# Gate columns in one stationary tile, gates of new tokens from a diagonal, decay rows of three heads by transfers

## The chip, the cores and the metric

One core of a Trainium2 chip runs the whole program. The engines are TensorE (PE, matmuls), VectorE (DVE), ScalarE (ACT) and GpSimd (POOL); SyncE (SP) issues most DMA transfers. The metric is the device time of one execution in microseconds; lower is better. Three runs of the kernel before took 1218.15, 1218.84 and 1219.11 us.

## The reference

One layer of a decoder trunk on 512 prompt tokens and 8 new tokens of other sequences: a SwiGLU feed-forward (FFN), a token mixer, a second FFN, each with norms around it. The mixer has two branches of four heads each, retention and gated DeltaNet. What the change touches is the gates of the DeltaNet branch (8 columns of `w_in`, 4 for `ga`, 4 for `gb`) and the decays made from them:

```python
proj = (h @ w_in).astype(f32)
rq, rk, rv, rg, conv_in, gz, ga, gb, gate_r, gate_g = jnp.split(proj, idx, axis=-1)
beta = jax.nn.sigmoid(gb)
g_gdn = -jnp.exp(gdn_a_log.astype(f32)) * jax.nn.softplus(ga + gdn_dt_bias.astype(f32))
...
G = jnp.cumsum(gc, axis=-1)          # within a chunk
dm = decay_masks(G)                  # exp(G_i - G_j) below the diagonal
a_mat = jnp.eye(c, dtype=jnp.float32) + jnp.where(strict, bc[..., :, None] * dm * kk, 0.0)
u_v = lax.linalg.triangular_solve(a_mat, bc[..., None] * vc, ...)
qk = jnp.einsum('nbhid,nbhjd->nbhij', qc, kc) * dm
```

Inputs and outputs are fp32, and everything is computed in fp32 or in two-part splits of it.

## The kernel before

Features lie on the partitions, the 520 tokens on the free axis in two halves of 260 columns. A weight is loaded as `raw`, and split into a high part `whi` (a ScalarE cast, L350) and a rest `wlo` (a VectorE subtraction, L351); the activations `xhl` are split in the same way. A product takes three passes for each tile of 128 features, L408 to L410: high by high, high by rest, rest by high. A pass is one matmul of a 128x128 stationary tile with 260 columns. The feed-forwards save multiplications by seven-product schemes (`sv`, `dn`), which the change leaves alone.

The mixer (L1023) projects in the order of `proj_order`: first GAB, a block of 128 columns of which 8 are the gates and 120 are zeros, then the columns CK, CQ, CV of the four DeltaNet heads, the retention's RQ, RK, RV, and the gating columns. `first_units` (L701) does GAB and head 0's CK together, first half, then second half, while the sums of the norm are still being made: `ss` (L471) adds the squares over the partitions, `rb` (L477) spreads the factor of the norm over the partitions again. The raw result of GAB is scaled by `rb` into `rows` (L1167). `gates` (L1170) transposes `rows`, makes `g` (here `gg`) and `beta` for each token on VectorE and ScalarE, and then one group of matmuls into the bank `gc`: the running sums `G` of the chunks, by the triangle `triu` (L1215), and for the eight new tokens each gate of each head spread over all partitions, by eight matmuls of 8 columns, four for `g` and four for `beta` (L1218).

`gdn_head` (L1368) is a generator, one for each head. `decays` (L1235) spreads head h's `G` over the partitions: four fp32 matmuls, one for a chunk, into the bank `gbc` (L1240). From it ScalarE makes `eg` (L1244), VectorE `DT` (L1247) and `ekd`. Later the head works through its chunks: `ks` (L1447) multiplies the state S, `pS` (L1457) gives its update, which VectorE adds to S (L1459).

The order of the work is written by hand. Projections run as passes, and every 6 passes are a tick (`tick`, L223), some 0.72 us. Generators such as `gdn_head` are spawned beside them, and each `yield n` lets n ticks pass before the generator's next instructions are issued. `LATER`, a table at the head of the file, moves single steps: its entry `("gdn_head", 1): {51: 1, 52: -3}` makes the 51st wait of head 1 a tick longer and the 52nd three shorter, so the entries count the yields of a generator. TURN (48 ticks) keeps the heads apart. Each engine then works its own list strictly in that order.

## Time and profile before

| | |
|---|---|
| time, median of 3 runs | 1218.84 us |
| lowest and highest | 1218.15 and 1219.11 us |
| profiled execution | span 1218.5 us; no time of its own beside the span |
| PE busy | 1189.1 us (98%) |
| DVE busy | 899.6 us (74%) |
| ACT busy | 573.7 us (47%) |
| POOL busy | 277.1 us (23%) |
| matmuls on PE | 9937 |
| granted TensorE clock, mean | 0.990 |

The span goes from the first to the last instruction of the profiled execution. A busy TensorE isn't one at its peak: matmuls overlap, and their ends are modelled, so a matmul is read by the distance from its start to the next one's start. A fp32 matmul appears as two records. The mixer's part that the change touches lies between about 366 and 650 us.

### The profile page before, as it was taken

The numbers are of one execution on the slowest core, as the hardware profiler recorded it, in microseconds if no ns is written. First come the engines' busy times: TensorE is split into PE (matmuls) and PEld (weight loads), VectorE is DVE, ScalarE is ACT, GpSimd is POOL, SyncE is SP. The second block draws the span as 40 slices with busy tenths as digits, with TensorE's granted clock in tenths as the row PEclk, the third lists the DMA queues.
The fourth block names the chain that finished last, engine by engine and source line by source line (L and its number), as shares of the span: only waits on it lengthen the run. The fifth ranks groups of instructions, "written<-read, shape, count | busy, mean of one in ns | idle before, by whom it ended". The sixth has DMA issues, their size and how long they took to land.

```text
span 1218.5 us, 25498 instructions
## 1 busy us (share of the span) xinstructions
PE 1189.1 (98%) x9937; PEld 1176.9 (97%) x9937; DVE 899.6 (74%) x1933; ACT 573.7 (47%) x1195; POOL 277.1 (23%) x502
## 2 busy tenths in 40 slices
PE   8999999999999999999999999999999999999995
PEld 7999999999999999999999999998999999999994
DVE  8988888776548787877666667546888888867554
...
DMA packets 79689, 170.87 MB, mean 140 GB/s; under 512 B 17104, under 2 KB 20016, under 8 KB 79568
## 3 DMA queue, kind: packets, MB, share of 16 engines
...
## 4 chain that ended last, share of the span: by engine, by line
PE 88%; DVE 6%; ACT 2%; issue 1%; DMA 1%; POOL 1%; SPq 0%; DVEq 0%; ACTq 0%; POOLq 0%
PE sv L408 10%; PE sv L409 10%; PE sv L410 10%; PE p L408 7%; PE p L410 7%; PE p L409 7%; PE dn L408 7%; PE dn L409 7%; PE dn L410 7%; DVE wlo L351 2%; PE br L408 1%; PE br L409 1%; PE br L410 1%; PE g L409 1%; PE g L410 1%
## 5 line engine op out<-in xcount | busy, mean ns | idle before, releaser
L408 PE MATMUL p<-xhl,whi 128*128 128x260 f32 x784 | 231.0, 295 | 0.0
L409 PE MATMUL p<-xhl,whi 128*128 128x260 f32 x784 | 222.0, 283 | 1.4 <-DVE xhl L506 1.4
L410 PE MATMUL p<-xhl,wlo 128*128 128x260 f32 x784 | 221.3, 282 | 1.7 <-DVE wlo L351 1.7
L351 DVE TENSOR_TENSOR wlo<-raw,whi 128x1024 fp32r<-128x1024 f32 (+2 forms) x121 | 142.3, 1182 | 37.7 <-ACT whi L350 35.9
L408 PE MATMUL sv<-th,w 128*128 128x260 f32 x592 | 167.2, 282 | 0.5 <-ACT q L833 0.5
L409 PE MATMUL sv<-tl,w 128*128 128x260 f32 x592 | 167.1, 282 | 0.0
L410 PE MATMUL sv<-th,w 128*128 128x260 f32 x592 | 167.0, 282 | 0.0
L409 PEld LDWEIGHTS p<-xhl,whi 128*128 128x128 f32 x784 | 148.4, 189 | 2.0 <-DVE xhl L506 1.8
L410 PEld LDWEIGHTS p<-xhl,wlo 128*128 128x128 f32 x784 | 147.9, 189 | 2.1 <-DVE wlo L351 2.1
L408 PEld LDWEIGHTS p<-xhl,whi 128*128 128x128 f32 x784 | 148.1, 189 | 0.7
L350 ACT CAST whi<-raw 128x1024 fp32r<-128x1024 f32 (+2 forms) x121 | 116.4, 971 | 31.3 <-DMA raw<-dn_in 16.9
L369 DVE TENSOR_TENSOR w<-s,w 128x512 fp32r<-128x512 f32 x148 | 101.5, 688 | 37.9 <-ACT w L368 36.5
L307 POOL DMA_DIRECT2D s<-gu_in x74 | 65.1, 973 | 282.4 <-DMA s<-gu_in 143.8
L410 PE MATMUL dn<-hh,wlo 128*128 128x260 f32 x448 | 126.6, 283 | 1.2 <-DVE wlo L351 1.2
L408 PE MATMUL dn<-hh,whi 128*128 128x260 f32 x448 | 127.0, 283 | 0.0
L409 PE MATMUL dn<-hl,whi 128*128 128x260 f32 x448 | 126.7, 283 | 0.0
L409 PE MATMUL sv<-xhl,w 128*128 128x260 f32 x444 | 125.5, 283 | 0.0
L408 PE MATMUL sv<-xhl,w 128*128 128x260 f32 x444 | 125.4, 282 | 0.0
L410 PE MATMUL sv<-xhl,w 128*128 128x260 f32 x444 | 125.0, 281 | 0.0
L408 PEld LDWEIGHTS sv<-th,w 128*128 128x128 f32 x592 | 111.4, 188 | 0.9 <-ACT q L833 0.7
L410 PEld LDWEIGHTS sv<-th,w 128*128 128x128 f32 x592 | 111.6, 188 | 0.0
L409 PEld LDWEIGHTS sv<-tl,w 128*128 128x128 f32 x592 | 111.2, 188 | 0.0
(408 smaller groups left out, 3230.4 us busy)
## 6 DMA issues: line engine op xcount, KB each, us to landing
...
s<-gu_in SPq DMA_DIRECT2D x74, 256.0 KB, 5.7
s<-gu_in POOLq DMA_DIRECT2D x74, 256.0 KB, 5.4
...
a<-gu_in SPq DMA_DIRECT2D x37, 256.0 KB, 5.9
...
```

The source lines that it names most:

```text
L307: self.nc.gpsimd.dma_start(out=out, in_=term, accum_op=ALU.add)
L350: self.nc.scalar.copy(hi[:, ks], t[:, ks])
L351: self.nc.vector.tensor_tensor(lo[:, ks], t[:, ks], hi[:, ks].bitcast(F32), ALU.subtract)
L369: nc.vector.tensor_tensor(w[:, 1], t[i], w[:, 0].bitcast(F32), ALU.subtract)
L408: mm(ps, hi[:, k, :], xh, start=first, stop=False, skip_group_check=more)
L409: mm(ps, hi[:, k, :], xl, start=False, stop=False, skip_group_check=more)
L410: mm(ps, lo[:, k, :], xh, start=False, stop=last, skip_group_check=more)
```

## The change

GAB is loaded as its 8 columns alone (`gab`, 32 KB and not 512 KB). A stationary tile `both` is filled with zeros by ScalarE, the high parts of the 8 columns go into its columns 0 to 7, and VectorE's rests into 8 to 15. It then takes two passes, by the high and by the low part of the activations, and the result has 16 rows, which are added in pairs in `gates` after the transposes.

For the new tokens `g` and `beta` are multiplied with an identity into a diagonal `dg`, and one matmul with a stationary tile of ones spreads all 64 numbers.

One further matmul gives `G` in rows (16 rows of 128, a row for each chunk and head). They are copied to SBUF and written to DRAM (`gscr`). Heads 1 to 3 have their rows spread by a transfer that SP issues ROWS_EARLY = 12 ticks before the decays; `eg` and `DT` then read SBUF. Head 0 keeps its four matmuls, which now stand in `gdn_head`. The transfer adds a yield to heads 1 to 3, so that the entries of `LATER` meet the yield before the one that they met so far.

```diff
@@ units: the order of the loads
-            out += [("win", i, 0, 8) for i in range(n)]
+            out += [("gab", 0, 0, 8)] + [("win", i, 0, 8) for i in range(n - 1)]
...
@@ load_to
+            elif u[0] == "gab":
+                t = self.slot("gabw", (P, KD, 8))
+                nc.sync.dma_start(out=t, in_=a["gab"])
...
@@ split
+        if self.unit_list[j][0] == "gab":
+            self.load_to(j)
+            t = self.loaded[self.group[j]]
+            both = self.whl.tile([P, KD, P], F32R, tag="w", name=self.name("both"))
+            self.started(j)
+            self.split_done[j] = (both, None)
+            self.nc.scalar.activation(both, self.ones.unsqueeze(1).to_broadcast([P, KD, P]), AF.Copy, scale=0.0)
+            self.nc.scalar.copy(both[:, :, 0:8], t)
+            self.nc.vector.tensor_tensor(both[:, :, 8:16], t, both[:, :, 0:8].bitcast(F32), ALU.subtract)
+            return
...
@@ passes
         mm(ps, hi[:, k, :], xh, start=first, stop=False, skip_group_check=more)
+        if lo is None:
+            mm(ps, hi[:, k, :], xl, start=False, stop=last, skip_group_check=more)
+            return
...
@@ gates
+        sb = c.tile([P, 5, 16], F32, name="gsb")
+        nc.gpsimd.memset(sb, 0.0)
...
-        nc.vector.tensor_tensor(ga[:, 0:4, :], ptv[:, 0:4, 0:4], dt.unsqueeze(1).to_broadcast([P, 4, H]), ALU.add)
-        nc.vector.tensor_tensor(ga[0:DEC, 4, :], ptv[0:DEC, 4, 0:4], dt[0:DEC], ALU.add)
-        nc.vector.tensor_copy(gb[:, 0:4, :], ptv[:, 0:4, 4:8])
-        nc.vector.tensor_copy(gb[0:DEC, 4, :], ptv[0:DEC, 4, 4:8])
+        nc.vector.tensor_copy(sb[:, 0:4, :], ptv[:, 0:4, :])
+        nc.vector.tensor_copy(sb[0:DEC, 4, :], ptv[0:DEC, 4, :])
+        nc.vector.tensor_tensor(ga, sb[:, :, 0:4], sb[:, :, 8:12], ALU.add)
+        nc.vector.tensor_tensor(gb, sb[:, :, 4:8], sb[:, :, 12:16], ALU.add)
+        nc.vector.tensor_tensor(ga, ga, dt.unsqueeze(1).to_broadcast([P, 5, H]), ALU.add)
...
+        diag = self.small("dg", [P, 2, H, DEC])
+        eye = self.ident[0:DEC, 0:DEC].unsqueeze(1).to_broadcast([DEC, H, DEC])
+        for i, src in enumerate((g, beta)):
+            nc.vector.tensor_tensor(diag[0:DEC, i], src[0:DEC, 4, :].unsqueeze(2).to_broadcast([DEC, H, DEC]), eye, ALU.mult)
         yield 13
 
         pc = self.bank("gc")
         nc.tensor.matmul(pc[:, 0:16], self.triu, g[:, 0:4, :], start=True, stop=True)
-        for i, src in enumerate((g, beta)):
-            for h in range(H):
-                nc.tensor.matmul(
-                    pc[:, 16 + (i * H + h) * DEC : 16 + (i * H + h + 1) * DEC],
-                    src[0:DEC, 4, h : h + 1].to_broadcast([DEC, P]),
-                    self.ident[0:DEC, 0:DEC],
...
+        nc.tensor.matmul(pc[0:16, P : 2 * P], g[:, 0:4, :], self.triu, start=True, stop=True)
+        nc.tensor.matmul(pc[:, 16:80], self.ones[0:DEC, :], diag[0:DEC], start=True, stop=True)
+        grow = self.slot("growc", (16, P))
+        nc.vector.tensor_copy(grow, pc[0:16, P : 2 * P])
+        self.gscr = self.dram.tile([NCH, H, P], F32, name="gscr")
+        nc.sync.dma_start(out=self.gscr.rearrange("c h i -> (c h) i"), in_=grow)
...
+    def decay_rows(self, h):
+
+        t = self.slot("gbc", (P, NCH, P))
+        self.nc.sync.dma_start(out=t, in_=self.gscr[:, h, :].unsqueeze(0).to_broadcast([P, NCH, P]))
+        return t
...
@@ gdn_head
-        if turn > self.now:
-            yield turn - self.now
-        eg, DT = self.decays(h)
+        if h:
+            if turn - ROWS_EARLY > self.now:
+                yield turn - ROWS_EARLY - self.now
+            rows = self.decay_rows(h)
+            yield max(turn, self.now + ROWS_EARLY) - self.now
+        else:
+            if turn > self.now:
+                yield turn - self.now
+            rows = self.bank("gbc").rearrange("p (c i) -> p c i", i=P)
+            for i in range(NCH):
+                nc.tensor.matmul(rows[:, i, :], self.g[:, i, h : h + 1].to_broadcast([P, P]), self.triu, start=True, stop=True)
+        eg, DT = self.decays(h, rows)
```

The order of the instructions changes with it. On TensorE at the gates (bank `gc`; `gbc` is head 0's decay rows, `p` the passes of a projection) the kernel before has:

```order
L410 MATMUL p_5735<-xhl_5177,wlo_5524 128x260
L1215 MATMUL gc_5748<-gg,cst 128x16
L1218 MATMUL gc_5748<-cst,gg 128x8 x4
L1218 MATMUL gc_5748<-cst,beta 128x8 x4
L1240 MATMUL gbc_5773<-cst,gg 128x128 x4
L408 MATMUL p_5734<-xhl_5010,whi_5523 128x260
```

The changed kernel has at the same place, with `dg` the diagonal:

```order
L427 MATMUL p_5723<-xhl_5169,wlo_5509 128x260
L1237 MATMUL gc_5736<-gg,cst 128x16
L1238 MATMUL gc_5736<-cst,gg 16x128
L1239 MATMUL gc_5736<-dg_5577,ones 128x64
L1433 MATMUL gbc_5759<-cst,gg 128x128 x4
L422 MATMUL p_5722<-xhl_5010,whi_5508 128x260
```

Eight matmuls have become two, and the passes are at L422, L426 and L427 now (L424 is the second pass of the gate columns).

On VectorE in head 1's third chunk (`S` the state, `pS` its update from TensorE, `sg` and `ol` the end of a retention head, `cv` the next chunk's values from `ks`), the kernel before has:

```order
L1481 TENSOR_TENSOR go_7241<-go_7241,gs_8151 128x512
L1459 SCALAR_TENSOR_TENSOR S_7949<-S_7949,egl_6471,pS_8296 128x128
L1468 COPY go_7950<-go_8299 128x128
L1615 COPY gor_8198<-cb_8305 128x32
L1666 COPY sp_7838<-sp_8312 128x8
L1588 SCALAR_TENSOR_TENSOR sg_8110<-tr_8322,vec,sg_8110 128x512
L1590 TENSOR_TENSOR ol_8328<-sg_8110,oh_8327 128x512
L1750 TENSOR_TENSOR on_dec_g<-gdo,gor_8198 128x32
L1624 COPY urow_8343<-tr_1402_8341 32x128
L1363 TENSOR_SCALAR ro_8130<-ro_8130,mv_8131,rsr_8280 128x128 x4
L1578 COPY sgd_8348<-sg_8260 128x8
L1448 SCALAR_TENSOR_TENSOR cv_5723<-ks_8382,neg_eg,cv_5723 128x128
```

and the changed kernel:

```order
L1510 TENSOR_TENSOR go_7221<-go_7221,gs_8128 128x512
L1644 COPY gor_8175<-cb_8273 128x32
L1695 COPY sp_7820<-sp_8280 128x8
L1617 SCALAR_TENSOR_TENSOR sg_8087<-tr_8290,vec,sg_8087 128x512
L1619 TENSOR_TENSOR ol_8296<-sg_8087,oh_8295 128x512
L1488 SCALAR_TENSOR_TENSOR S_7926<-S_7926,egl_6454,pS_8306 128x128
L1497 COPY go_7927<-go_8309 128x128
L1779 TENSOR_TENSOR on_dec_g<-gdo,gor_8175 128x32
L1653 COPY urow_8320<-tr_1403_8318 32x128
L1477 SCALAR_TENSOR_TENSOR cv_5711<-ks_8332,neg_eg,cv_5711 128x128
```

The S update now stands behind `sg` and `ol`. On TensorE the three matmuls `pS`, `go`, `go` have moved behind the transposes that `sg` reads and 6 passes, and `ks`, which needs S, follows them after 6 passes; so far 30 passes stood between `pS` and `ks`.

On SP, where head 1's rows are loaded (`raw` a weight load, `s` a scratch write of the head before it), the kernel before has:

```order
L287 DMA raw_6050<-win_in 128x1024
L287 DMA raw_6126<-win_in 128x1024
L287 DMA raw_6239<-win_in 128x1024
L287 DMA raw_6327<-win_in 128x1024
L287 DMA raw_6435<-win_in 128x1024
L1493 DMA s_1089_6473<-AT_6400 32x4x32 x4
```

and the changed kernel:

```order
L291 DMA raw_6036<-win_in 128x1024
L291 DMA raw_6112<-win_in 128x1024
L1257 DMA gbc_6178<-gscr 128x4x128
L291 DMA raw_6227<-win_in 128x1024
L291 DMA raw_6315<-win_in 128x1024
L291 DMA raw_6418<-win_in 128x1024
```

The transfer of the rows stands between two weight loads, behind the one that was `raw_6126` before.

## Rows read from the trace of the kernel before

**Rows 1.** The page: chain that ended last, shares by engine

```profile
PE 88%; DVE 6%; ACT 2%; issue 1%; DMA 1%; POOL 1%; SPq 0%; DVEq 0%; ACTq 0%; POOLq 0%
```

**Rows 2.** Windows: length; PE, PEld, DVE, ACT, POOL busy; clock, DMA share, GB/s

```profile
370.00:374.00 4.00, 2.97 (x24) 2.64 (x25) 4.00 (x10) 1.85 (x5) 2.90 (x4) 1.00 0.63 155
```

**Rows 3.** Timeline of PE: start, us, line, operation [idle before, releaser]

```profile
393.57 1.02 PE L471 MATMUL ss<-ones,sq 128*87 128x1 f32 x12
```

**Rows 4.** Timeline of DVE, squares of the norm and its factor

```profile
387.89 5.17 DVE L537 TENSOR_TENSOR sq<-sq,sq 128x520 f32<-128x520 f32 x7
...
398.78 0.43 DVE L557 COPY rb<-rb 128x260 f32<-128x260 f32 x1 [1.72 <-PE rb L477]
```

**Rows 5.** Timeline of PE, a wait for a weight split

```profile
412.45 0.39 PE L410 MATMUL p<-xhl,wlo 128*128 128x260 f32 x1 [1.40 <-DVE wlo L351]
```

**Rows 6.** Timeline of PE at the gates and behind them

```profile
420.64 1.05 PE L1218 MATMUL gc<-cst,gg 8*128 8x8 f32 x8
421.55 1.03 PE L1218 MATMUL gc<-cst,beta 8*128 8x8 f32 x8
422.51 2.08 PE L1240 MATMUL gbc<-cst,gg 128*128 128x128 f32 x8
424.25 0.57 PE L408 MATMUL p<-xhl,whi 128*128 128x260 f32 x1
424.61 0.42 PE L409 MATMUL p<-xhl,whi 128*128 128x260 f32 x1
424.82 0.42 PE L410 MATMUL p<-xhl,wlo 128*128 128x260 f32 x1
```

**Rows 7.** Windows around the gates, columns as in rows 2

```profile
418.00:422.00 4.00, 4.00 (x37) 3.97 (x35) 2.59 (x13) 3.96 (x7) 0.19 (x1) 1.00 1.05 369
...
423.00:424.00 1.00, 1.00 (x7) 1.00 (x7) 0.96 (x3) 1.00 (x9) 0.00 (x0) 0.50 1.03 381
...
426.00:427.00 1.00, 1.00 (x10) 1.00 (x10) 0.39 (x2) 0.65 (x2) 1.00 (x3) 1.00 0.89 160
```

**Rows 8.** Timeline of PE at head 1's decay rows

```profile
463.05 1.05 PE L1240 MATMUL gbc<-cst,gg 128*128 128x128 f32 x8
463.86 0.37 PE L408 MATMUL p<-xhl,whi 128*128 128x260 f32 x1
464.06 0.28 PE L409 MATMUL p<-xhl,whi 128*128 128x260 f32 x1
464.18 0.28 PE L410 MATMUL p<-xhl,wlo 128*128 128x260 f32 x1
```

**Rows 9.** Timeline of DVE behind the gates

```profile
430.93 0.16 DVE L1226 COPY gcol<-gc 128x16 f32<-128x16 f32 x1
...
441.14 0.60 DVE L1418 SCALAR_TENSOR_TENSOR qk<-pa,rr,DT 128x128 f32<-128x128 f32 x2
```

**Rows 10.** Timeline of PE, the pass into the bank behind `qk`

```profile
443.87 0.29 PE L408 MATMUL p<-xhl,whi 128*128 128x260 f32 x1
```

**Rows 11.** The DMA view: issues, KB each, us to landing

```profile
rb<-urow SPq DMA_DIRECT2D x8, 256.0 KB, 5.5
...
s<-AT SPq DMA_DIRECT2D x16, 16.0 KB, 3.2
```

**Rows 12.** Timeline of SP, the weight load ahead of head 1's rows

```profile
457.34 0.33 SPq L287 DMA_DIRECT2D raw<-win_in  x1
```

**Rows 13.** Timeline of ACT, head 1's first use of its rows

```profile
468.60 0.60 ACT L1244 ACTIVATE eg<-gbc 128x512 f32<-128x512 f32 x1
```

**Rows 14.** Groups of DVE instructions by shape: busy, mean ns, idle before

```profile
L1643 DVE SCALAR_TENSOR_TENSOR sd<-rb,gkn,sd 128x128 f32<-128x128 f32 x32 | 9.0, 343 | 0.0
...
L1247 DVE SCALAR_TENSOR_TENSOR DT<-gbc,gcol,cst 128x128 f32<-128x128 f32 x16 | 4.5, 341 | 0.5 <-ACT eg L1244 0.5
```

**Rows 15.** Timeline of DVE in head 1's third chunk

```profile
604.02 0.69 DVE L1590 TENSOR_TENSOR ol<-sg,oh 128x512 fp32r<-128x512 f32 x1 [0.74 <-ACT oh L1589]
```

**Rows 16.** Timeline of PE in head 1's third chunk

```profile
606.03 0.38 PE L1447 MATMUL ks<-S,cv 128*128 128x128 f32 x2
```

More of the change, by code (lines that the diff above doesn't have):

```diff
@@ L36 @@
 TURN = 48
+ROWS_EARLY = 12
 WARM = 9
@@ L1166, in gate_rows @@
         for hf, (c0, n) in enumerate(HALVES):
-            self.nc.vector.tensor_tensor(rows[0:8, c0 : c0 + n], ps[hf][0:8], self.r[hf][0:8], ALU.mult)
+            self.nc.vector.tensor_tensor(rows[0:16, c0 : c0 + n], ps[hf][0:16], self.r[hf][0:16], ALU.mult)
         return rows
@@ L1233, in gates, with decays @@
         self.ekd = c.tile([P, NCH, H], F32, name="ekd")
-    def decays(self, h):
-        nc = self.nc
-        pb = self.bank("gbc")
-        for i in range(NCH):
-            nc.tensor.matmul(
-                pb[:, i * P : (i + 1) * P], self.g[:, i, h : h + 1].to_broadcast([P, P]), self.triu, start=True, stop=True
-            )
+    def decay_rows(self, h):
+        t = self.slot("gbc", (P, NCH, P))
+        self.nc.sync.dma_start(out=t, in_=self.gscr[:, h, :].unsqueeze(0).to_broadcast([P, NCH, P]))
+        return t
+    def decays(self, h, pb):
+        nc = self.nc
         eg = self.slot("eg", (P, NCH, P))
@@ L1248, in decays @@
                 out=dt[:, i, :],
-                in0=pb[:, i * P : (i + 1) * P],
+                in0=pb[:, i, :],
                 scalar=self.gcol[:, i, h : h + 1],
@@ L1256, in decays @@
         e = self.ekd[:, :, h]
-        nc.vector.tensor_tensor(e, pb.rearrange("p (c i) -> p c i", i=P)[:, :, P - 1], self.gcol[:, :, h], ALU.subtract)
+        nc.vector.tensor_tensor(e, pb[:, :, P - 1], self.gcol[:, :, h], ALU.subtract)
         nc.scalar.activation(e, e, AF.Exp)
@@ L1795, in layouts @@
         if kind == GAB:
-            b = np.zeros((D, P), f)
-            b[:, 0:8] = w[:, 4096:4104]
-        else:
-            b = w[:, start[kind] + h * P : start[kind] + (h + 1) * P]
+            out["gab"] = asc(w[:, 4096:4104].reshape(KD, P, 8).transpose(1, 0, 2))
+            continue
+        b = w[:, start[kind] + h * P : start[kind] + (h + 1) * P]
         blocks.append(b.reshape(KD, P, P).transpose(1, 0, 2))
```

13 lines of the change are left out of this document (4 added, 9 removed).

## The prediction

> **What bounds the kernel now.** First the chain that ended last [rows 1]: 88% of the span is TensorE matmul, VectorE follows with 6%. So an edit is worth what it takes from TensorE's instruction stream, unless TensorE then meets a VectorE result that isn't ready. I therefore read, for each of the four places that the change touches, TensorE's timeline, and beside it VectorE's timeline with the rows that TensorE waits for next.
>
> 1. Start of the mixer, first half: between 370 and 374 VectorE is busy 4.00 of 4.00 us and TensorE 2.97 [rows 2]. TensorE is the one that waits.
> 2. Second half: TensorE runs without a gap up to the sums `ss` at 393.57 [rows 3], whose input VectorE finishes at 387.89 + 5.17 = 393.06 [rows 4]. From there the work is one chain: `ss`, VectorE's copy of `rb` (it sat idle 1.72 us for it at 398.78, [rows 4]), VectorE's rows and convolutions, and TensorE's wait of 1.40 us for a weight split at 412.45 [rows 5].
> 3. The gates at 420: sixteen tiny matmuls, then head 0's decay rows, then ordinary passes [rows 6], and a fall of the granted clock to 0.50 (1.2 GHz) for 422.5 to 426 [rows 7].
> 4. The decay rows `gbc` of heads 1 to 3, in the middle of TensorE's passes [rows 8]; head 1's stands here, the others look alike.
>
> An ordinary pass starts 0.12 us after the one before (464.06, 464.18, [rows 8]).
>
> **The change part by part.** The profiled execution has a span of 1218.5 us and no other time of its own; the median of the runs is 1218.84, 0.34 above. I work in differences and subtract them from the median.
>
> *Gate columns.* 16 passes go, 8 in each half. First half: 8 × 0.12 = 0.96 us, but VectorE is full there and TensorE waits for it, so 0 (at most 0.96). Second half: 0.96 us, but `ss` can come forward only to VectorE's last square, 393.57 − 393.06 = 0.51. I take 0.45, as a hand-over takes a little. The chain behind carries this 0.45 whole, through the wait at 412.45, since VectorE's part of it starts with `rb`. Bounds 0 and 1.92. The smaller load and the zero filling lie far before, beside the previous FFN's passes; a subtraction of 64 columns replaces one of 1024 there, and I count nothing.
>
> *Gate matmuls.* The sixteen run from 420.64 to 422.51 = 1.87 us [rows 6]. In their place stand one matmul with 128 moving columns and one with 64. Head 1's four 128-column fp32 matmuls took 0.81 us [rows 8], so 0.20 each; two come to 0.40, and I take 0.45. Saved: 1.42. Bounds: 1.0, if each new one were to cost twice that, to 1.6.
>
> *The clock.* TensorE is busy 4.00 of 4.00 us from 418 to 422 at clock 1.00, and yet the clock falls right after the tiny matmuls and is 0.50 in 423 to 424 [rows 7]. What they have in particular is that only 8 columns move in each. What the fall costs: head 0's decay rows last 424.25 − 422.51 = 1.74 us, head 1's 0.81, so 0.93; and from 424.25 to 426 passes come every 0.21 us (424.61, 424.82) and not 0.12, so (1 − 0.12/0.21) × 1.75 = 0.75. Together 1.68 us. With the sixteen gone I expect no fall: the 1.40 us of idleness before 412.45 caused none, and the new pair plus `gbc` is a shorter stretch of small work than that before. Bounds 0 and 1.7. The Trainium skill, "TensorE: Matmul & The Clock Gate" (Part 1: The HAM clock gate), has the clock follow how busy the engine has been, low by default and after idleness. Read by busy time it disagrees with the rows, since the engine wasn't idle before the fall; by it the sixteen wouldn't be the cause, and the fall would stay. That is a rival below.
>
> *What VectorE lets through.* So far TensorE would be 0.45 + 1.42 + 1.68 = 3.55 us early from 426 on. VectorE is busy there nearly without a gap and waits for ScalarE, not for TensorE, from 412 to 443, so it comes forward only by the 0.45. It also gets more to do: one more small operation at the gates, a copy `growc` and two diagonals of 8×32. A small copy is 0.16 us (`gcol`, [rows 9]). Two of these lie in gaps where it waits for ScalarE; I count 0.30 for the rest. So VectorE comes 0.15 earlier. At 443.87 a pass starts [rows 10] in a bank that VectorE frees with `qk`, at 441.14 + 0.60 = 441.74 [rows 9]: a slack of 2.13 us. TensorE can be at most 2.13 + 0.15 = 2.28 us early there; 3.55 − 2.28 = 1.27 is given back as a new wait between 434 and 444. I keep 2.28. Bounds 1.5 (VectorE gets 0.8 us of extra work in its way) and 3.55.
>
> *Three heads' rows.* Each head loses 0.81 us of matmul plus 0.08 of the first pass behind it (463.86 to 464.06 is 0.20 and not 0.12, [rows 8]): 0.89; a little less where the neighbours are closer, so 0.87 × 3 = 2.6. In exchange SP issues a 256 KB load for each. For head 1 it stands behind a weight load issued at 457.34, which occupies SP for 0.33 [rows 12], and ScalarE wants the rows at 468.60 [rows 13]: 468.60 − 457.67 = 10.9 us of cover. The nearest row by bytes, the broadcast `rb<-urow`, lands in 5.5 us; the nearest by pieces, `s<-AT` (16 KB in 128 runs of 32 numbers), takes 3.2, which for 512 runs would make 12.8 at worst [rows 11]. I take 5.5: the row has the same size and the same broadcast. So the load is hidden by 5 us, and 12.8 would make head 1 late by 1.9. VectorE and ScalarE now read the rows from SBUF: an operation of that kind and size takes 343 ns from SBUF and 341 from PSUM [rows 14], nothing. Bounds of the three heads: 2.6 gained, or 0 if VectorE is the limit at each.
>
> *The order behind.* The extra yield shifts heads 1 and 2 in the tables. In head 1 `ks` follows its S update after 6 passes and not after 30, and 18 passes that stood between the transposes and `ks` fall behind it; VectorE does the S update behind `ol`. TensorE would be at `ks` at 606.03 − 18 × 0.12 = 603.87 [rows 16]. `ol` starts at 604.02 and takes 0.6 until the next can start [rows 15]; it comes 0.4 earlier, as three matmuls ahead of the transposes and two VectorE operations are gone from before it. So S starts at 604.2 and is done at 604.5: a wait of 0.6, and I take +0.5 (0 to 1.5). In head 2 similar moves cost or save some 0.2; I count nothing.
>
> Sum: −2.28 − 2.6 + 0.5 = −4.4, so 1218.84 − 4.4 = 1214.4.
>
> **The rivals.**
>
> A. *Nothing is given back.* VectorE's chain behind 426 moves along, and head 1 stays without a wait: −3.55 − 2.6 = −6.2, 1212.7. For it: the tiny matmuls also held up transposes that ScalarE and VectorE use. Against: VectorE's gaps in 412 to 443 end on ScalarE.
>
> B. *The clock falls all the same* (what the page's rule amounts to). Then TensorE is early by 0.45 + 1.42 = 1.87 only, below the cap of 2.28, and nothing is given back: −1.87 − 2.6 + 0.5 = −4.0, 1214.9. The fall costs hardly more than what VectorE would take anyway.
>
> C. *VectorE becomes the limit through all the heads.* It follows TensorE by 2 us at 444; if each head's 0.87 runs into the next wait for it, only the first part stays: −2.28 + 0.5 = −1.8, 1217.0. For it: the slack at 444 is used up by then. Against: VectorE has its own idle time later, and its splits wait for ScalarE.
>
> D. *The decay rows come late* (slower). The place is ScalarE's `eg` of heads 1 and 2. If a load takes T, each is late by T − 10.9, taking head 1's cover for both, and everything of the head waits in order behind it on ScalarE and VectorE. With the 4.4 won elsewhere it decides from 2 × (T − 10.9) = 4.4, T = 13.1, and is slower by 0.2% from T = 14.3. At T = 17 it is +12.2 − 4.4 = +7.8, 1226.6. For it: runs of 512 bytes, and a queue on which loads wait for buffers. Against: both rows named lie below 13.
>
> **How the numbers follow.** 0.2% of the median is 2.44 us, about what a measurement can tell from no change: faster means below 1216.4, slower above 1221.3. My case 0.47 (1213.6 to 1215.8 by itself), A 0.15, B 0.12, C 0.20, D 0.06. My case, A and B are faster; C is faster in its better half and the same otherwise, and of D a little ends as the same. Faster 0.77 (0.47 + 0.15 + 0.12 + 0.03), same 0.18, slower 0.05. The range holds A below and C above: 1211.9 to 1217.4.
>
> **What would show it.** Right: no drop of the clock at 422 to 426; gate matmuls in under 0.6 us; a new wait of TensorE for VectorE of 1 to 1.6 us between 434 and 444; heads 1 to 3 with no `gbc` on TensorE and ScalarE's `eg` not waiting for a transfer; `ks` of head 1 waiting about 0.5 us for S. Wrong: `eg` waiting for the load of `gbc`, or a clock of 0.50 behind the gates, or new VectorE waits of a microsecond or more in each head.

## The result, and the profile after

The changed kernel took 1223.72 us, the median of 4 runs (1222.93 to 1224.37), beside 1218.55 for the kernel before (4 runs, 1218.15 to 1219.11): a ratio of 1.0046, 95% interval 1.0031 to 1.0060. It is slower by 5.2 us, where 4.4 us faster was predicted, and outside the predicted range. The profiled execution is the run of 1222.93, with a span of 1221.1.

The executions of one kernel differ by 1 to 6 us, so the accounts below set the trace of after against `ctrl`, the kernel before run once more with a profile (1217.76, span 1216.0), at the same instruction of TensorE. "Lag" is how much later after has it.

The page's chain that ended last, shares by engine, answers to [rows 1]: TensorE has fallen from 88% to 79%, and VectorE has risen from 6 to 10.

```profile
PE 79%; DVE 10%; ACT 4%; POOL 3%; issue 2%; DMA 1%; SPq 0%; DVEq 0%; ACTq 0%; POOLq 0%
```

Timeline of TensorE in after at the gates (start, us, line, operation), which answers to [rows 6]:

```profile
418.89 0.40 PE L1237 MATMUL gc<-gg,cst 128*128 128x16 f32 x2
419.22 0.39 PE L1238 MATMUL gc<-cst,gg 128*16 128x128 f32 x2
419.54 0.43 PE L1239 MATMUL gc<-dg,ones 8*128 8x64 f32 x2
419.90 1.16 PE L1433 MATMUL gbc<-cst,gg 128*128 128x128 f32 x8
420.81 0.37 PE L422 MATMUL p<-xhl,whi 128*128 128x260 f32 x1
421.02 0.28 PE L426 MATMUL p<-xhl,whi 128*128 128x260 f32 x1
421.14 0.28 PE L427 MATMUL p<-xhl,wlo 128*128 128x260 f32 x1
```

The two new matmuls take 419.90 − 419.22 = 0.68 us where the tiny ones took 1.87 (eight matmuls of two records each; the prediction counts the records and says sixteen), and passes follow 0.12 apart. At 425.9 TensorE is 4.2 us ahead of the trace of before. But 1.3 us of this stand already at 366, ahead of everything that the change touches here: that execution of before lies 1.2 us behind `ctrl` from 30 us on. The change itself brought 2.9 us up to here (3.55 predicted). Then TensorE is stopped. The view of waits, TensorE of after (us in total, times, longest), has two rows of over 1 us to which before has nothing alike:

```profile
PE cb L1643 <- POOL gdm L1640: 2.0, 1, 2.0
...
PE tr L1179 <- DVE dgb L1248: 1.8, 1, 1.8
```

**The first stop, 431.** Timeline of ScalarE in after; a bracket gives the idle time before and what ended it:

```profile
430.08 1.28 ACT L1247 ACT_TABLE_LOAD   x1 [3.35 <-DVE gcol L1245]
431.37 0.20 ACT L1247 ACTIVATE dgb<-gc 128x32 f32<-128x32 f32 x1
...
469.06 0.63 ACT L1264 ACTIVATE eg<-gbc 128x512 f32<-128x512 f32 x1
```

The same in before:

```profile
428.04 1.28 ACT L1228 ACT_TABLE_LOAD   x1
431.12 0.20 ACT L1228 ACTIVATE dgb<-gc 128x32 f32<-128x32 f32 x1 [1.80 <-DVE gcol L1226]
```

In before the activation table is loaded while ScalarE would wait for VectorE anyway. In after `dgb` has two waits, one for TensorE and one for VectorE's `gcol`, and the second stands on the load, as the load's own bracket shows. The load starts only behind `gcol`, and its 1.28 us come after the wait and not beside it. VectorE then waits 1.60 for ScalarE and TensorE 1.78 for VectorE.

**The second stop, 498.** Timeline of GpSimd in after:

```profile
451.60 1.11 POOL L1543 TENSOR_TENSOR pack<-pack 128x31 f32<-128x31 f32 x1
...
453.10 0.24 POOL L1543 TENSOR_TENSOR pack<-pack 128x30 f32<-128x30 f32 x1
...
494.55 1.12 POOL L1316 COPY rdec<-rp 128x8 f32<-128x8 f32 x1 [1.64 <-DVE rp L1315]
...
497.99 0.57 POOL L1640 TENSOR_TENSOR gdm<-gdm,mhalf 64x1 f32<-64x1 f32 x1
```

Timeline of VectorE in after, two of the weight splits:

```profile
451.34 1.26 DVE L365 TENSOR_TENSOR wlo<-raw,whi 128x1024 fp32r<-128x1024 f32 x1
...
494.40 1.22 DVE L365 TENSOR_TENSOR wlo<-raw,whi 128x1024 fp32r<-128x1024 f32 x1
```

Timeline of TensorE in after, the two stops and head 1's `ks`:

```profile
431.85 0.66 PE L1179 MATMUL tr<-cst,cv 128*128 128x128 f32 x4 [1.78 <-DVE dgb L1248]
...
498.61 0.43 PE L1643 MATMUL cb<-cst,gdm 64*128 64x64 f32 x2 [2.04 <-POOL gdm L1640]
...
604.94 0.49 PE L1476 MATMUL ks<-S,cv 128*128 128x128 f32 x2 [0.32 <-DVE S L1488]
```

GpSimd works its list in order: the steps of head 0's triangular inverse (`pack`), copies such as `rdec`, and then `gdm`, which the decode's `cb` on TensorE needs. In before it looked like this (GpSimd, then TensorE):

```profile
497.33 0.57 POOL L1611 TENSOR_TENSOR gdm<-gdm,mhalf 64x1 f32<-64x1 f32 x1
```

```profile
498.44 0.43 PE L1614 MATMUL cb<-cst,gdm 64*128 64x64 f32 x2
```

`gdm` ended at 497.90 and TensorE came at 498.44: a slack of 0.54 (1.05 in `ctrl`). Against this trace GpSimd of after delivers 0.66 us later, and TensorE, which would have been at `cb` at 496.57, comes 1.9 us earlier. Against `ctrl` TensorE has no lead any more at this place: it comes 0.9 later, and GpSimd 3.95 later. The same rows of `ctrl` (SP and GpSimd, then TensorE; `s` and `L` carry a head's inverse problem through DRAM to GpSimd):

```profile
440.03 2.39 SPq L1493 DMA_DIRECT2D s<-AT  x4
443.98 1.23 SPq L1499 DMA_DIRECT2D L<-s  x2
447.38 0.24 POOL L1513 TENSOR_TENSOR pack<-L,pack 128x31 f32<-128x31 f32 x1 [0.32 <-DMA L<-s]
494.04 0.57 POOL L1611 TENSOR_TENSOR gdm<-gdm,mhalf 64x1 f32<-64x1 f32 x1
495.66 0.43 PE L1614 MATMUL cb<-cst,gdm 64*128 64x64 f32 x2
```

and of after:

```profile
441.52 1.77 SPq L1522 DMA_DIRECT2D s<-AT  x4
447.28 1.23 SPq L1528 DMA_DIRECT2D L<-s  x2
450.76 0.76 POOL L1542 TENSOR_TENSOR pack<-L,pack 128x31 f32<-128x31 f32 x1 [2.21 <-DMA L<-s]
```

VectorE's `AT` of head 0 starts 1.48 later than in `ctrl`, behind the first stop, and the transfer `s` is issued 1.49 later. `L` follows `s` by 5.76 us and not by 3.95, so that GpSimd's first step is 3.38 late; its further steps add 0.57. So the first stop is a part of the second one. Why `L` came later was not tested; before has 5.26 there, with its own instructions.

The rows also show why GpSimd isn't ahead, in any of these traces: a step that takes 0.24 us alone takes 1.11 when it meets a `wlo` of VectorE, and ends with it (451.34 + 1.26 = 452.60, 451.60 + 1.11 = 452.71); `rdec` is held until 495.67 by the one that ends at 495.62. The Trainium skill has this in "SBUF — State Buffer" (Who interferes with whom): a VectorE instruction with two SBUF inputs contends with a GpSimd one that reads SBUF, the shared ports are an exclusive lock, and the order of issue decides which of the two is blocked. The rows agree.

**The clock.** Windows of after (length; PE, PEld, DVE, ACT, POOL busy; clock, DMA share, GB/s):

```profile
422.00:424.00 2.00, 2.00 (x19) 2.00 (x18) 1.98 (x3) 2.00 (x15) 0.42 (x1) 1.00 0.62 234
...
500.00:502.00 2.00, 2.00 (x25) 1.96 (x25) 1.94 (x6) 1.94 (x5) 1.19 (x5) 0.72 0.71 244
502.00:504.00 2.00, 2.00 (x11) 2.00 (x11) 1.90 (x6) 0.70 (x3) 1.76 (x5) 0.50 0.06 16
```

The fall at 422 is gone; 2.3 us behind the wait at `cb` there is one to 0.50 (1.2 GHz) that before has not. And here is `ctrl`, the kernel before once more, where [rows 7] had a fall:

```profile
422.00:424.00 2.00, 2.00 (x20) 2.00 (x19) 1.97 (x3) 2.00 (x15) 1.45 (x1) 1.00 0.81 302
424.00:426.00 2.00, 2.00 (x20) 2.00 (x19) 1.28 (x6) 1.18 (x3) 2.00 (x4) 1.00 0.60 119
```

No fall, by the same instructions. What [rows 7] showed belongs to some of the executions.

**Where the 5.1 us of span went**, by the lag of after behind `ctrl` at the same TensorE instruction:

| from, to (us in `ctrl`) | lag behind it | this stretch | what is in it |
|---|---|---|---|
| to 419.08, last pass before `gc` | −0.51 | −0.51 | gate columns: −0.54 at `ss` |
| 421.30, `gbc` | −1.40 | −0.89 | gate matmuls −1.20; `gc` comes some 0.3 later, its weight load having waited 0.25 for VectorE's `cin` |
| 431.27, `tr` | +0.58 | +1.98 | the wait for `dgb`, 1.78 |
| 460.03 | +1.21 | +0.63 | VectorE behind it, 0.50 of it up to 441.57 |
| 461.28 | +0.33 | −0.88 | head 1's decay rows |
| 495.45 | +0.84 | +0.51 | 0.39 of it in one stop (at 474.90 in after) |
| 495.66, `cb` | +2.95 | +2.11 | the wait for `gdm`, 2.04 |
| 501.17 | +4.50 | +1.55 | the clock's fall |
| 505.86 | +3.61 | −0.89 | head 2's decay rows |
| 566.02 | +4.13 | +0.52 | 0.38 of it a wait for VectorE's `pack` (at 514.75 in after) |
| 595.96 | +3.34 | −0.79 | head 3's decay rows, −0.90 at their place |
| 603.62 | +3.93 | +0.59 | the shifted order of heads 1 and 2 |
| 840.13 | +4.69 | +0.76 | the rest of the mixer, whose instructions are the same |
| 978.07 | +5.05 | +0.36 | second FFN, whose instructions are the same |

The stretch of the order ends where both kernels have done the same work: `ctrl` has `pS`, `go`, `go` (0.67 us) already at 596.2, after only behind `cb`.

### The profile page after: what moved, and what is told of

Its sections match the earlier page's. It is cut to its first block, busy times and chain, and to the rows that moved or that the text cites. A ratio compares the mean times of both kernels' runs of the same rounds, so it can differ in the third digit from the quotient of the medians.

```text
span 1221.1 us, 25398 instructions
## 1 busy us (share of the span) xinstructions
PE 1186.9 (97%) x9885; PEld 1172.7 (96%) x9885; DVE 901.6 (74%) x1937; ACT 573.6 (47%) x1196; POOL 276.6 (23%) x501
## 3 DMA queue, kind: packets, MB, share of 16 engines
q8 instruction: 77, 1.26, 0.4%
## 4 chain that ended last, share of the span: by engine, by line
PE 79%; DVE 10%; ACT 4%; POOL 3%; issue 2%; DMA 1%; SPq 0%; DVEq 0%; ACTq 0%; POOLq 0%
PE sv L422 10%; PE sv L426 10%; PE sv L427 10%; PE dn L422 7%; PE dn L427 7%; PE dn L426 7%; PE p L422 5%; PE p L426 5%; PE p L427 5%; DVE wlo L365 2%; PE br L422 1%; PE br L426 1%; PE br L427 1%; ACT whi L364 1%; PE sp L1694 1%
## 5 line engine op out<-in xcount | busy, mean ns | idle before, releaser
L422 PE MATMUL p<-xhl,whi 128*128 128x260 f32 x768 | 227.1, 296 | 0.2
L427 PE MATMUL p<-xhl,wlo 128*128 128x260 f32 x768 | 218.0, 284 | 1.8 <-DVE wlo L365 1.8
L426 PE MATMUL p<-xhl,whi 128*128 128x260 f32 x768 | 218.0, 284 | 0.0
L422 PE MATMUL sv<-th,w 128*128 128x260 f32 x592 | 167.5, 283 | 0.5 <-ACT q L850 0.5
L426 PE MATMUL sv<-tl,w 128*128 128x260 f32 x592 | 167.3, 283 | 0.0
L427 PE MATMUL sv<-th,w 128*128 128x260 f32 x592 | 167.0, 282 | 0.0
L427 PEld LDWEIGHTS p<-xhl,wlo 128*128 128x128 f32 x768 | 145.7, 190 | 2.2 <-DVE wlo L365 2.2
L422 PEld LDWEIGHTS p<-xhl,whi 128*128 128x128 f32 x768 | 145.4, 189 | 1.3 <-DVE u L1314 0.3
L426 PEld LDWEIGHTS p<-xhl,whi 128*128 128x128 f32 x768 | 146.0, 190 | 0.0
L427 PE MATMUL dn<-hh,wlo 128*128 128x260 f32 x448 | 126.8, 283 | 1.2 <-DVE wlo L365 1.2
L422 PE MATMUL dn<-hh,whi 128*128 128x260 f32 x448 | 127.1, 284 | 0.0
L426 PE MATMUL dn<-hl,whi 128*128 128x260 f32 x448 | 126.6, 283 | 0.0
L422 PE MATMUL sv<-xhl,w 128*128 128x260 f32 x444 | 125.5, 283 | 0.0
L426 PE MATMUL sv<-xhl,w 128*128 128x260 f32 x444 | 125.5, 283 | 0.0
L427 PE MATMUL sv<-xhl,w 128*128 128x260 f32 x444 | 125.4, 283 | 0.0
L422 PEld LDWEIGHTS sv<-th,w 128*128 128x128 f32 x592 | 111.3, 188 | 0.8 <-ACT q L850 0.7
L427 PEld LDWEIGHTS sv<-th,w 128*128 128x128 f32 x592 | 111.7, 189 | 0.0
L426 PEld LDWEIGHTS sv<-tl,w 128*128 128x128 f32 x592 | 111.4, 188 | 0.0
```

What stands on the lines that cost most here:

```text
L422: mm(ps, hi[:, k, :], xh, start=first, stop=False, skip_group_check=more)
L426: mm(ps, hi[:, k, :], xl, start=False, stop=False, skip_group_check=more)
L427: mm(ps, lo[:, k, :], xh, start=False, stop=last, skip_group_check=more)
```

## The experiments

Times are medians, with the range and the number of runs, and the ratio to the kernel before run beside it with its 95% interval. Each kernel's clock is read from one profiled execution.

**How far the kernel before repeats.** `ctrl` is the kernel before, unchanged.

> The kernel before, unchanged, as a control. The changed kernel's times lie 1.8 us above their spans (1222.93 against 1221.1), the kernel before showed 1218.84 and a span of 1218.5, which need not be of the same execution. If the kernel before also lies about 1.8 above its span, its span in ordinary runs is near 1216.8, and the change costs about 5 us inside the span; if it lies 0.3 above, 1.4 us of the 5.2 us are outside the span and belong to how the program is started or ended. Ratio 1.000 in both cases.

Measured: 1219.32 (1217.76 to 1220.54, 10), 1.0006 [0.9997, 1.0015]. The kernel differs from itself by up to 2.8 us between executions, and its profiled one has no fall at 422. Its time lies 1.8 us above its span, as that of the changed kernel does, so the loss lies inside the span. By this estimate the execution of before that was profiled (span 1218.5) took some 1220.3, more than the three runs that the prediction set beside it.

**One part alone.** `gabonly` is the kernel before with the gate columns' part, `diagonly` with the diagonal, `rowsonly` with the rows by transfers.

```diff
gabonly
+            self.nc.scalar.copy(both[:, :, 0:8], t)
+            self.nc.vector.tensor_tensor(both[:, :, 8:16], t, both[:, :, 0:8].bitcast(F32), ALU.subtract)
diagonly
+        nc.tensor.matmul(pc[:, 16:80], self.ones[0:DEC, :], diag[0:DEC], start=True, stop=True)
rowsonly
+        self.nc.sync.dma_start(out=t, in_=self.gscr[:, h, :].unsqueeze(0).to_broadcast([P, NCH, P]))
```

> The kernel before with the gate columns' part of the change alone (one stationary tile, two passes, gates added in pairs); eight gate matmuls and the matmuls of the decay rows stay. Theory one (the loss lies in a second chain, VectorE, transfer, GpSimd's inverse, that the decay rows' part makes later): dgb has a single wait, nothing is late, TensorE gains 0.5 us at the sums and the time is 1218.0 within 0.7. Theory two (the slower passes of the second feed-forward, 119.47 to 120.0 ns in every version with the whole change, come with this part, because it moves tiles in the memory): 119.9 ns or more there, and 1.2 us more, 1219.2.

> The kernel before with the diagonal alone: one matmul of 64 columns for the eight of 8 columns. TensorE's part at the gates falls from 1.87 us to about 1.0 without the second new matmul, dgb keeps its single wait. Theory one: TensorE is early by 1.2 to 1.6 us at 421, GpSimd's chain is not, so that little remains: 1217.9 within 0.7. Rival (TensorE's early start is kept to the end): 1216.9. Second feed-forward at 119.47 ns.

> The kernel before with the decay rows' part alone: rows by a matmul, a copy and transfers for heads 1 to 3, the shifted table of waits included. Theory one: ScalarE's table load waits for VectorE's growc and gcol, dgb is 1.3 to 1.5 us late, GpSimd's chain with it; TensorE waits about 1 to 2 us at cb and heads 1 to 3 save 2.6: 1220 to 1221.5, most of the loss of the whole change. Rival (this part pays, the loss belongs to the others): 1216 or less. If the order of heads 1 and 2 costs, the stretch from 597 to 607 us is 1 us longer or more than in the kernel before.

Measured: `gabonly` 1221.13 (1220.65 to 1222.62, 9), 1.0025 [1.0016, 1.0035]; `diagonly` 1220.70 (1217.73 to 1222.40, 10), 1.0015 [1.0004, 1.0025]; `rowsonly` 1220.73 (1219.41 to 1222.46, 10), 1.0019 [1.0009, 1.0029]. Each part alone costs time, though each takes work from TensorE. The times of the first two lie outside all that was expected; that of `rowsonly` came as theory one had it, but without its wait: TensorE waits 0.03 at `cb`, and not 1 to 2. `gabonly` waits 0.9 us at `cb`; its windows show two falls of the clock that `ctrl` has not:

```profile
372.00:374.00 2.00, 2.00 (x12) 2.00 (x12) 1.49 (x5) 1.25 (x4) 1.57 (x3) 0.54 0.00 0
374.00:376.00 2.00, 2.00 (x14) 2.00 (x12) 1.55 (x2) 2.00 (x3) 0.65 (x1) 0.61 0.00 0
...
500.00:502.00 2.00, 2.00 (x12) 2.00 (x11) 1.86 (x7) 0.37 (x2) 1.69 (x6) 0.54 0.25 35
```

The windows of `ctrl` in the first of these places:

```profile
372.00:374.00 2.00, 2.00 (x21) 2.00 (x20) 1.71 (x4) 1.15 (x3) 1.84 (x3) 1.00 0.00 0
```

`diagonly` has a fall at 566 to 570, `rowsonly` the one at 422 to 427, and it pays 0.59 for the order at 596 to 604, where 1 or more was to show that it costs.

**The load of the gate columns.** `gabin` reads the 8 columns out of a block of `win` instead of an input of their own.

```diff
-                nc.sync.dma_start(out=t, in_=a["gab"])
+                nc.sync.dma_start(out=t, in_=a["win"][0, :, 0, 0:64].rearrange("p (k g) -> p k g", g=8))
```

> The changed kernel, but the 8 gate columns are not an input of their own: they stand in a block of the weight array that was there before, and are loaded from it. If the extra input costs time outside the span, the time falls by up to 1.4 us and the span stays at 1221 to 1222.6. If not, the time stays at 1223.7 within 0.7 us.

Measured: 1224.40 (1221.67 to 1226.56, 4), 1.0047 [1.0029, 1.0065]: the same as after. The additional input isn't it.

**The first stop repaired.** In `growlast` the copy of G's rows stands behind `gcol`, `dgb` and `neg_eg`.

```diff
-        grow = self.slot("growc", (16, P))
-        nc.vector.tensor_copy(grow, pc[0:16, P : 2 * P])
...
         nc.vector.tensor_scalar(self.neg_eg, self.neg_eg, -1.0, None, ALU.mult)
+        grow = self.slot("growc", (16, P))
+        nc.vector.tensor_copy(grow, pc[0:16, P : 2 * P])
```

> The changed kernel, but VectorE copies the rows growc after gcol, dgb and neg_eg and not ahead of them. ScalarE's dgb then needs to wait for VectorE alone, as before the change; so far its second wait stands on the table load ahead of it, so that the load of 1.28 us begins only after gcol (430.08) and not in idle time (428.04 before). Theory one (this late load holds up VectorE, the decays of head 0, and with them GpSimd's chain): dgb moves from 431.60 to about 430.1, everything of head 0 and GpSimd's chain come 1.3 us earlier, TensorE's wait at cb stays near 2 us because TensorE is let go earlier too, and the time falls by about 1.3 to 1222.4. Rival (GpSimd's chain starts by the transfers of the solve and not by the decays): the wait at cb grows by 1.3 and the time stays at 1223.7.

Measured: 1224.01 (1222.70 to 1225.32, 4), 1.0045 [1.0030, 1.0060]. ScalarE loads its table early again:

```profile
427.28 1.28 ACT L1243 ACT_TABLE_LOAD   x1
430.37 0.20 ACT L1243 ACTIVATE dgb<-gc 128x32 f32<-128x32 f32 x1 [1.80 <-DVE gcol L1241]
```

TensorE's wait at `tr` falls from 1.78 to 0.52, so the cause of that wait is shown. The wait at `cb` stays at 2.08, as theory one had it: counted from the last pass before the gates, TensorE gets past `cb` 1.56 us earlier than in after, and GpSimd delivers that much earlier. So the first stop does delay GpSimd's chain. The time doesn't fall by 1.3 all the same. In the profiled execution the gain goes later: some 1.0 in a fall of the clock at 601 to 605, which after has not, and 0.5 behind 1080.

**The second stop moved.** `cblater` lets the decode's `cb` come 3 ticks later; `growlast_cb` is both. `pooloff` has GpSimd's two output transfers issued by SP, and `allfix` has `growlast`, `pooloff` and the entries of `LATER` moved to the yields that they met before.

```diff
cblater, growlast_cb
-    ("decode_gdn", 0): {1: 8, 2: 2, 10: 3},
+    ("decode_gdn", 0): {1: 8, 2: 2, 3: 3, 10: 3},
pooloff, allfix
-        nc.gpsimd.dma_start(out=self.a["cprm"], in_=self.cprm)
+        nc.sync.dma_start(out=self.a["cprm"], in_=self.cprm)
allfix
-    ("gdn_head", 1): {0: 3, 51: 1, 52: -3},
+    ("gdn_head", 1): {0: 3, 52: 1, 53: -3},
```

> The changed kernel with one number more in the table of shifts: the matmul cb that reads GpSimd's gdm is issued 3 ticks (18 passes, 2.2 us) later. Theory one (GpSimd's chain of inverse steps is late and TensorE, which runs ahead of it, waits 2.04 us at cb; the idleness is what lowers the clock behind it): the wait and the fall of the clock at 501 to 505 go, 3 to 4 us in all, about 1220. Theory two (the fall of the clock comes from the small matmuls cb and pV that stand there, not from the wait): only the 2.0 us of the wait go, about 1221.7. Theory three (TensorE is only moved against GpSimd's next results): it waits at the next one, and the time stays within 1 us of 1223.7.

> The whole change with both repairs: growc copied last, so that the table load is free, and cb 3 ticks later. Each alone left 1224.0 and 1222.6. Theory one: together they take away the wait at cb (2.0 us) and 1.3 us of the late start, and no idleness of 2 us is left that could lower the clock: 1220 to 1221. Rival (GpSimd's chain is what counts, wherever TensorE waits for it): the same as the later cb alone, 1222.6 within 0.7, with the wait at po.

> The whole change, with one thing taken off GpSimd: the two output transfers cprm and cdec, which it issues ahead of gdm (0.66 + 1.08 us), are issued by SP. Theory one (GpSimd's chain of inverse steps arrives at 495 to 498 later than TensorE, and TensorE's earliness turns into a wait there, behind which the clock falls): gdm comes about 1.7 us earlier, the wait of 2.04 us at cb shrinks to about 0.3, the fall of the clock behind it goes, and the time falls by 2 to 4 us, to 1220 to 1221.5. Rival (the waits are a symptom, and what is lost is lost elsewhere): 1223.7 within 1 us.

> The whole change with three repairs: growc copied last (table load free), the table of shifts moved by one entry for heads 1 and 2 (the order of the kernel before), and cprm and cdec issued by SP. Theory one: 1.7 us off GpSimd, 1.3 us off the start of its chain, 0.65 us off ks: no wait of more than 0.5 us at cb and no fall of the clock, 1218 to 1219; the second feed-forward stays at 120.0 ns, which holds 1.2 us back. Rival: 1222 or more, as each repair alone gave nothing or 1 us.

Measured: `cblater` 1222.60 (1220.33 to 1223.61, 7), 1.0032 [1.0021, 1.0044]; `growlast_cb` 1222.52 (1222.07 to 1223.80, 5), 1.0035 [1.0022, 1.0048]; `pooloff` 1224.13 (1222.91 to 1225.33, 4), 1.0050 [1.0035, 1.0065]; `allfix` 1221.76 (1219.24 to 1224.94, 10), 1.0033 [1.0023, 1.0043]. A later `cb` moves the wait to `po` (1.6 and 2.0), which waits for GpSimd too. The profiled execution of `cblater` has no fall of the clock between 366 and 650, and its span (1220.0) is still 4.0 above that of `ctrl`: most of the loss doesn't need one. In `pooloff` `gdm` is not earlier: GpSimd stands still 3.51 us for `rp` ahead of `rdec`, in place of 1.64. So it isn't GpSimd's own load that holds `gdm` but what stands ahead of it, waiting for VectorE.

**That copy taken away.** `rdecdve` is after, `bdec` before, `alldec` is `allfix`, each with `rdec<-rp` on VectorE.

```diff
-        nc.gpsimd.tensor_copy(self.rdec[:, 0 if kind == RQ else 1, h, :], out[:, SEQ:TOK])
+        nc.vector.tensor_copy(self.rdec[:, 0 if kind == RQ else 1, h, :], out[:, SEQ:TOK])
```

> The changed kernel, with the copy `rdec<-rp` (128x8) issued on VectorE instead of GpSimd. Theory: TensorE's wait of 2.04 us at `cb` is GpSimd's queue: GpSimd stands still 1.64 us at 494.55 for VectorE's `rp`, takes 1.12 us for this copy, and `gdm` stands behind it. With the copy gone, `gdm` comes up to 2.8 us earlier, the wait at `cb` falls from 2.04 to under 0.5, and the time falls by 1.5 to 2, and by 1.9 more if the clock then doesn't fall at 501: 1219.8 to 1222.2. Rival: VectorE is what TensorE meets next; `gdm` comes earlier, a wait for VectorE of about the same length follows within 10 us, and the time stays within 1 of 1223.7.

> The kernel before, with the same copy on VectorE. Theory: TensorE reaches `cb` 0.5 to 1.05 us after `gdm` there, so an earlier `gdm` is worth nothing: 1218.2, within 0.8, and eight small copies more on VectorE are hidden. Rival: GpSimd's queue already held the kernel before somewhere, and it gains over 1.5.

> The changed kernel with all repairs: the copy of G's rows behind `gcol` and `dgb`, the entries of LATER moved by one yield, GpSimd's two output transfers issued by SP, and the copy `rdec<-rp` on VectorE. Theory: no wait over 0.5 at `cb`, none over 0.6 at `tr`, heads as in the prediction, with 1.2 lost in the second FFN: 1215.5 to 1217.5. Rival: another wait for VectorE in its place between 495 and 510, 1220 or more, as with the repairs without the last one (1221.76).

Measured: `rdecdve` 1222.14 (1219.94 to 1223.76, 11), 1.0027 [1.0018, 1.0035]; `bdec` 1218.95 (1217.75 to 1222.61, 12), 1.0009 [0.9999, 1.0018]; `alldec` 1220.03 (1218.03 to 1221.71, 11), 1.0011 [1.0003, 1.0020]. The wait at `cb` falls from 2.04 to 0.35 in `rdecdve`:

```profile
497.63 0.43 PE L1643 MATMUL cb<-cst,gdm 64*128 64x64 f32 x2 [0.35 <-POOL gdm L1640]
```

No fall of the clock follows it, from 461 to 506 its lag behind `ctrl` grows by 0.95 where that of after grew by 3.28, and the medians of `rdecdve` and `alldec` lie 1.6 and 1.7 below those of after and `allfix`. The kernel before gains nothing by the same edit, having had slack there. This is the theory's case for the second stop. The growth between 461 and 506 is the better evidence: part of the 1.6 can come from the second FFN, where `rdecdve` has faster passes (below). In `alldec` GpSimd itself sits idle before `gdm`, for VectorE:

```profile
496.22 0.55 POOL L1640 TENSOR_TENSOR gdm<-gdm,mhalf 64x1 f32<-64x1 f32 x1 [2.73 <-DVE gdm L1638]
```

`cb` waits 0.44 there, `tr` 0.63. The expectation of 1215.5 to 1217.5 failed all the same, and the time is in the rival's range: falls of the clock at 372 to 380 and 600 to 606 stand in the profile, and `po` waits 0.50 for VectorE at 502.

**The rows alone, repaired; and without the gate columns.** `rowsfix` is `rowsonly` with the copy last and `LATER` moved; `rowsdiagfix` adds the diagonal to it, `rowsdiagdec` also `rdec` on VectorE.

```diff
rowsfix, rowsdiagfix, rowsdiagdec
-    ("gdn_head", 2): {0: 3, 33: 5, 44: -5, 49: 2},
+    ("gdn_head", 2): {0: 3, 34: 5, 45: -5, 50: 2},
rowsdiagfix, rowsdiagdec
+        nc.tensor.matmul(pc[:, 16:80], self.ones[0:DEC, :], diag[0:DEC], start=True, stop=True)
rowsdiagdec
+        nc.vector.tensor_copy(self.rdec[:, 0 if kind == RQ else 1, h, :], out[:, SEQ:TOK])
```

> The kernel before with the decay rows' part alone, growc copied last and the order of heads 1 and 2 as before. Against the part without the two repairs (1220.7) theory one takes off 1.3 us for the table load and 0.65 for ks: 1218.5 to 1219. Rival (TensorE gets nothing from the three heads because GpSimd's chain ends when it did): the same as the kernel before, 1218.1, or 0.5 above.

> The change without its gate columns part (GAB stays 128 columns and three passes), repaired: copy of G's rows last, LATER moved by one yield, `rdec<-rp` on VectorE. Theory: the fall of the granted clock at 372 to 380, which 5 of 10 profiled executions with the gate columns part show and none of 8 without it, comes from that part, and so does its cost; and without the sixteen tiny matmuls there is none at 422. So no fall in either place; 1.2 at the gates and 2.6 at the heads are kept, less up to 1.2 in the second FFN and up to 1.9 for a fall at 600: 1214.5 to 1217.5. Rival: the losses of the changed kernel come from the rows and the diagonal, and this one stays at 1219 to 1221 as alldec (1220.03).

> As rowsdiagdec, with `rdec<-rp` on GpSimd as in the kernel before. Theory: TensorE comes to `cb` 1.2 us earlier than in the kernel before, which was there 0.5 to 1.05 after `gdm`; so it waits 0.2 to 0.7 for it: 0.2 to 0.7 slower than rowsdiagdec, 1215 to 1218. Rival: GpSimd's queue doesn't count here, both are the same within 0.2.

Measured: `rowsfix` 1219.02 (1217.56 to 1221.43, 10), 1.0006 [0.9997, 1.0016]; `rowsdiagdec` 1219.37 (1217.80 to 1221.58, 11), 1.0007 [0.9998, 1.0016]; `rowsdiagfix` 1224.06 (1220.94 to 1224.19, 5), 1.0038 [1.0024, 1.0052]. No fall at 372 nor, with the diagonal, at 422; in their place `rowsdiagdec` and `rowsdiagfix` show falls at 566 to 570 and 600 to 605, where the expectation allowed for one. The time of `rowsdiagdec` is in the rival's range. The windows of `rowsfix` at 600:

```profile
600.00:602.00 2.00, 2.00 (x14) 1.95 (x14) 0.92 (x2) 0.51 (x1) 1.53 (x7) 0.65 0.06 9
602.00:604.00 2.00, 2.00 (x12) 2.00 (x11) 1.86 (x7) 1.58 (x3) 1.63 (x5) 0.50 0.41 66
```

`rowsdiagfix` and `rowsdiagdec` differ by the one copy, and by 4.7 us, where 0.2 to 0.7 was expected. The direction fits; the size isn't explained. The profiled execution of `rowsdiagfix` is its shortest (1220.94), and `cb` waits there 0.76 for GpSimd (0.44 in `rowsdiagdec`):

```profile
495.64 0.43 PE L1626 MATMUL cb<-cst,gdm 64*128 64x64 f32 x2 [0.76 <-POOL gdm L1623]
```

The runs of 1224 have no trace. The edit also gives 89 later tiles another buffer, so the two don't differ in the copy alone.

**The second FFN and what precedes it.** `place` adds 320 bytes of constants to the kernel before, which shifts every later address alike; `ringshift` takes one unused tile from the buffers of the activations, so that every tile behind it lies in another one.

```diff
place
+        room = c.tile([P, 5, 16], F32, name="room")
+        nc.gpsimd.memset(room[:, 0, 0:1], 0.0)
ringshift
+        self.nc.vector.memset(self.slot("turned", (P, TOK))[0:1, 0:1], 0.0)
```

> The kernel before with one more constant of 320 bytes in each partition, set once by GpSimd (one element), so that nearly all tiles behind it lie 320 bytes further, as they do in the versions with the gate columns' part; nothing else is changed. If the place of the tiles makes the passes of the second feed-forward slower, they start 119.9 ns or more apart there (119.47 before), and the time is 1219.3. If not, 119.47 and 1218.1 within 0.7; then it is the order in which buffers are taken, or the work itself.

> The kernel before, with one unused tile taken from the buffers that the activations lie in, at the gates (and one memset of a single number). Every tile behind it lies in another buffer than before; the instructions stay. Theory: the distance between passes in the second FFN hangs on which buffers its tiles lie in: it goes from 119.46 to 119.9 to 120.1 ns between 900 and 1075, and the time rises by about 1.2, to 1219.4. Rival: the buffers don't matter, the distance stays at 119.46 within 0.05 and the time at 1218.2.

Measured: `place` 1218.30 (1217.39 to 1220.42, 10), 1.0005 [0.9996, 1.0014]; `ringshift` 1218.50 (1217.81 to 1220.21, 11), 1.0002 [0.9994, 1.0011]. The mean distance of passes between 900 and 1075 us is 119.46 ns in `ctrl`, 119.45 in `place`, 119.47 in `diagonly`, but 119.92 in `ringshift`, as in after (120.01), `gabonly` (119.92) and `rowsonly` (120.08), which all take other buffers. The buffers alone do this. TensorE of `ringshift` lags by 0.09 at 900 and by 0.78 at 1080; the 1.2 expected in the time isn't there. Moving `rdec` to VectorE gives 79 tiles of `bdec` and 89 of `rdecdve` another buffer than in before and after, and they show 119.92 and 119.38. So the buffers set the distance, up or down; which property of them does, was not found. Between 665 and 790, in the mixer, the ten kernels with the gate columns' part have 120.15 to 120.34 and the ten without it 119.58 to 119.79, `place` and `ringshift` among these. That is most of the 0.76 in the table above; its cause was not tested.

**The clock over all profiled executions.** How many show a fall in a place, among the kernels with and without a part (20, one execution each):

| place (us) | with | without |
|---|---|---|
| 372 to 380 | gate columns: 5 of 10 | 0 of 10 |
| 422 to 427 | the eight tiny matmuls: 4 of 8 | 0 of 12 |
| 498 to 511 | gate columns: 5 of 10 | 0 of 10 |
| 566 to 570 | the diagonal without the gate columns: 3 of 3 | 0 of 17 |
| 600 to 606 | rows by transfers: 7 of 13 | 0 of 7 |

Between 366 and 650 the five kernels with the instructions of before (`bdec`, `place` and `ringshift` among them) have 2 falls in 5 executions, the fifteen with a part of the change 23 in 15. One of these stands in no row of the table (`growlast_cb`, 555 to 559). At 1.55 us for one (the row of 501.17 above), 1.1 falls more in an execution are at most 1.7 us, an estimate from that row. Not every fall costs so much: `gabin`, `gabonly` and `growlast` fall at 372 to 377 and still gain the 0.78 on `ctrl` between 371 and 392 that after gains without a fall. No mended kernel beats the kernel before; the falls, the passes that lie further apart and the waits that are left stand against them, as far as the traces show. That the parts cause the falls rests on these counts alone, and most places and parts were picked from the traces. For 498 to 511 there is a rival: all five falls stand behind a wait of TensorE for GpSimd of 0.94 to 2.09 us. Against it, `pooloff` waits 2.10 at `cb` and `cblater` 1.6 at `po` without a fall.

## Why the prediction was wrong

- *What TensorE saves* was right in kind and nearly in size. Gate columns: 0.45 predicted, 0.54 at `ss` and 0.51 at the last pass before the gates. Gate matmuls 1.42, measured 1.20, of which `gc`, coming later, gives back some 0.3. Three heads 2.6, measured 0.88 + 0.89 + 0.90 = 2.67. The transfers were hidden: SP issued head 1's at 457.99, `eg` at 469.06 waited for none. Rival D, the only one on the slower side, did not happen.
- *The clock*, 1.68, is the first failed term. Its size was right: between 420 and 424 before falls 1.57 behind `ctrl`. The fall went, but of the 8 kernels with those matmuls only 4 show it in their profiled execution, so about half of it was there to be won; and others came. Rival B, by the rule of the Trainium skill, "TensorE: Matmul & The Clock Gate" (Part 1: The HAM clock gate), that idleness lets the clock fall, had the place wrong. The fall at 501 does follow a wait of 2.04 us, but no fall follows the wait of 1.78 at 431, nor that of 2.10 in `pooloff`; the runs don't settle that rule.
- *What VectorE lets through* is the step that failed. It had VectorE come 0.15 earlier and capped TensorE's lead once, by VectorE's `qk` at 443.87, keeping 2.28. Instead a reordered wait brought the table load of 1.28 into the way at 431: TensorE waited 1.78 for `dgb`, and VectorE came 1.48 later than in `ctrl`. What hangs on VectorE, two transfers and GpSimd's chain, was not looked at: it came 3.95 later at 498, where TensorE waited 2.04 at `cb`. The trace of before showed GpSimd done only 0.54 ahead there. With that cap the sum would have been −0.54 for all before 498, −1.74 for heads 2 and 3 and +0.5: 1217.1, no change, and still without GpSimd's delay. Missing was the search for the last arrival in *every* stage that the lead passes, and for what the change does to that arrival.
- *The order behind*, 0.5 (0 to 1.5), measured 0.59. At `ks` TensorE waited 0.32.
- *The passes behind*, in the rest of the mixer and the second FFN, weren't a term: 0.76 + 0.36 = 1.12.

Against the sum of −4.4, the table's +5.05 is made of these: the two stops, VectorE behind the first and the clock's fall, 1.98 + 0.63 + 2.11 + 1.55 = 6.27 in place of 1.27 given back, 5.00 more; the clock's 1.68, not to be had from `ctrl`; the small stops and slower passes of the heads, 0.51 + 0.52 + 0.11 = 1.14; the passes behind, 1.12; and 0.49 from the savings and the order. Together 9.43.
